# Partial sums of the modulation vectors: an accumulator in SBUF or in a bank of PSUM

## The chip, the cores and the metric

The kernel runs on one core of a Trainium2 chip, as one program in one launch. The metric is the device time of that core in microseconds. A profile is one execution taken by the hardware profiler; its span runs from the first to the last instruction.

## The reference

Two blocks of two layers each work on 256 tokens of width 1024. The second block is conditioned: a vector c of 1024 numbers passes through silu and is multiplied by `ada_w` (1024 x 6144 for each layer), which gives six modulation vectors of 1024 for each layer:

```python
mod = (c_act @ ada_w[l] + ada_b[l]).reshape(B, 6, D)[:, :, None, :]
sh1, sc1, g1, sh2, sc2, g2 = (mod[:, i] for i in range(6))
h = rmsnorm(x, norm_mix[l]) * (1 + sc1) + sh1
...
x = x + g2 * peer(h, peer_w_q[l], peer_sub_keys[l], peer_u[l], peer_v[l])
```

PEER picks 16 of 16384 experts for each of 8 heads of each token, weighs each by a gate, and returns the weighted sum of the experts' rows of `peer_v`. The kernel computes it densely: activations of all experts by `peer_u`, gates that are zero for most, and then the product with all of `peer_v`.

## The kernel before, in words

**Value phase.** Each PEER layer ends with a phase that multiplies the gated activations (128 slots of 128 experts x 256 tokens, in the SBUF tiles slots and slotb) by the 16384 rows of `peer_v`. It has 128 units of 128 experts. Products are made to nearly float32 accuracy from three passes of rounded halves (hi*whi, hi*wlo, lo*whi). In a unit:

- SyncE loads two units' rows at a time, 1 MB, into one of two raw buffers (line 331), when all readers of the buffer's old content are done;
- ScalarE rounds the rows to hi (128 x 1024, line 159), GpSimd subtracts to give one half of lo in two pieces of 256 columns (line 261), VectorE the other half (line 263, 512 columns); hi and lo have two buffers each, so this runs one unit ahead;
- ScalarE rounds the gated activations to whi, VectorE subtracts to give wlo (helper `split`, line 494), also one unit ahead;
- TensorE runs 12 matmuls of 512 columns (line 2093) into four banks of PSUM that are held for the whole phase (tag mm).

Nothing else on TensorE runs in the phase but a few small products.

**Modulation sums.** The generator `ada` (from line 640) computes 512 columns at a time of `c_act @ ada_w`: SyncE loads 256 rows x 512 columns (512 KB, line 654) into one of four buffers, three loads ahead; VectorE multiplies each 128 x 512 half by the entries of c (one scalar per partition) and adds it to an accumulator of 128 x 512. The first of eight such steps is a plain product (line 677), the other seven add (line 679). Then the accumulator is transposed in blocks of 32 (line 687) and reduced (line 688), and at the end of a call four small matmuls and an addition of the bias finish the vectors:

```python
elif first:
    nc.vector.tensor_scalar(out=acc, in0=x, scalar1=s, scalar2=None, op0=ALU.mult)
else:
    nc.vector.scalar_tensor_tensor(out=acc, in0=x, scalar=s, in1=acc, op0=ALU.mult, op1=ALU.add)
```

The generator `ada_slots` makes three such calls, of 2, 6 and 6 column blocks (14 in all: the last two of the first layer's vectors and all of the second layer's), in the first PEER layer's value phase, from unit 21 on. All their buffers lie in the part of the SBUF tile slots whose experts are already consumed. After them it makes the rotary angles.

**Order.** The order of instructions on each engine is written out by the program: after each unit's matmuls the planner (`tick`) grants the generators 1150 ns, and each `yield` of theirs states what the step before it is taken to cost, 660 ns for a sum. So sums are placed in VectorE's order between the subtractions of successive units, and VectorE executes them in that order.

**Banks of PSUM.** Of eight banks four have the tag mm, two aux, two s. `bank(tag)` gives the next buffer of that tag; an instruction that uses it waits until the readers of its old content are done. In the value phase the aux banks serve the small products of `ada`; the s banks were last used by the gates, in the phase before, and are used next by `back` after the phase.

Of the kernel before, what the change touches and what calls it, by code (L numbers as in the profile page):

```python
# [117 lines left out]
class _Kernel:  # L118
# [592 lines left out]
    def ada_slots(self, l):  # L711

        sl = self.slots
        while self.v_done < 21:
            yield 660.0
        for k, p0, n in ((l - 1, 10, 2), (l, 0, 6), (l, 6, 6)):
            yield from self.ada(k, p0, n, [sl[:, 1024 * i:1024 * (i + 1)] for i in range(4)], sl[:, 4096:4608],
                                sl[:, 4608:5120], sl[:, 5120:5248])
        yield from self.angles(sl)

# [1567 lines left out]
```

## Time and profile before

| | us |
|---|---|
| median of 3 runs | 2355.63 |
| lowest, highest | 2337.91, 2359.87 |
| profiled execution | 2348.06 |
| its span | 2346.3 |

Over the span TensorE is busy 2209.1 us, VectorE 1802.1, GpSimd 1744.4 and ScalarE 1295.0. The value phases lie at about 950 to 1340 us (first layer, the one with modulation sums) and 1975 to 2332 us (second layer). In a row of the profile, `L679 DVE SCALAR_TENSOR_TENSOR slots<-slots,cact` is VectorE's instruction of line 679, which writes a tile of the name slots and reads slots and cact. PE is TensorE, PEld its weight loads, DVE VectorE, ACT ScalarE, POOL GpSimd, SPq the queue of SyncE.

### The profile page before, as it was taken

How to read it: one execution, taken by the hardware profiler on the slowest of the kernel's cores; microseconds unless marked ns; L12 is line 12 of the kernel's file. 1: busy time of each engine (PE TensorE's matmuls, PEld its weight loads, DVE VectorE, ACT ScalarE, POOL GpSimd, SP SyncE). 2: the span in 40 equal slices, each digit the busy share in tenths (PEclk: the TensorE clock that was granted, in tenths of full speed). 3: DMA queues.
4: the chain of work that ended last, by engine and by line, in shares of the span. 5: the costliest groups of instructions: out<-in, count | busy, mean ns of one | idle time of the engine just before them, and what ended most of it. 6: DMA issues, size and time to landing. Idle time of an engine off the chain costs nothing. (4 is left out here: it accounts for less than half of the span.)

```text
span 2346.3 us, 42145 instructions
## 1 busy us (share of the span) xinstructions
PE 2209.1 (94%) x14789; PEld 1970.5 (84%) x14789; DVE 1802.1 (77%) x3502; ACT 1295.0 (55%) x2608; POOL 1744.4 (74%) x2070
## 2 busy tenths in 40 slices
PE   8998997899989999999998988998999999999997
PEld 7777887898989999877676777998889999888886
DVE  5818887578787999688989776697868998555555
ACT  2424674554437888544443554554448887555554
POOL 1107878788999888766675686568899888777776
PEclk9989998999999999999999999999999999999999
DMA  5326755477878877577878533587878876555554
GB/s 162 108 73 220 244 177 181 130 196 150 171 151 166 160 158 154 176 251 266 290 262 279 183 117 99 163 180 145 171 154 164 160 154 153 197 194 190 189 192 142
DMA packets 285583, 414.88 MB, mean 177 GB/s; under 512 B 16490, under 2 KB 217387, under 8 KB 285371
## 3 DMA queue, kind: packets, MB, share of 16 engines
q1 hardware_dynamic: 279722, 405.30, 63.6%
q10 hardware_dynamic: 5648, 6.89, 1.1%
q8 instruction: 116, 1.90, 0.4%
q14 instruction: 97, 0.79, 0.1%
HBM read 408.98 MB, written 3.15 MB: 176 GB/s over the span
## 5 line engine op out<-in xcount | busy, mean ns | idle before, releaser
L261 POOL TENSOR_TENSOR lo<-raw,hi 128x256 fp32r<-128x256 f32 x956 | 887.2, 956 | 401.1 <-ACT hi L159 380.4
L261 POOL TENSOR_TENSOR lo<-uT,hi 128x256 fp32r<-128x256 f32 x1022 | 779.0, 799 | 81.7 <-ACT hi L159 81.2
L159 ACT ACTIVATE hi<-raw 128x1024 fp32r<-128x1024 f32 x380 | 401.7, 1059 | 448.5 <-DMA raw<-in_peer_v 212.1
L2042 PE MATMUL mm<-h,hi 128*128 128x256 f32 x4096 | 530.5, 282 | 19.0 <-ACT hi L159 17.7
L2042 PEld LDWEIGHTS mm<-h,hi 128*128 128x128 f32 x4096 | 504.0, 189 | 23.0 <-ACT hi L159 20.5
L263 DVE TENSOR_TENSOR lo<-raw,hi 128x512 fp32r<-128x512 f32 (+1 forms) x290 | 231.2, 798 | 229.2 <-ACT hi L159 227.9
L231 DVE STREAM_TRANSPOSE uT<-raw 128x1024 f32<-128x1024 f32 x256 | 316.8, 1237 | 103.7 <-POOL lo L261 81.0
L159 ACT ACTIVATE hi<-uT 128x1024 fp32r<-128x1024 f32 x256 | 271.5, 1061 | 213.1 <-DVE uT L231 195.2
L2042 PE MATMUL mm<-h,lo 128*128 128x256 f32 x2048 | 313.1, 289 | 14.6 <-POOL lo L261 11.4
L2093 PE MATMUL mm<-hi,wlo 128*128 128x512 f32 x1024 | 278.7, 393 | 15.5 <-DVE wlo L494 15.5
L2042 PEld LDWEIGHTS mm<-h,lo 128*128 128x128 f32 x2048 | 263.5, 189 | 28.7 <-POOL lo L261 28.3
L2093 PE MATMUL mm<-hi,whi 128*128 128x512 f32 x1024 | 277.8, 392 | 5.4 <-ACT hi L159 4.9
L2093 PE MATMUL mm<-lo,whi 128*128 128x512 f32 x1024 | 276.0, 391 | 2.2 <-POOL lo L261 2.1
L2093 PEld LDWEIGHTS mm<-hi,wlo 128*128 128x128 f32 x1024 | 189.3, 188 | 67.0 <-DVE wlo L494 28.8
L2093 PEld LDWEIGHTS mm<-hi,whi 128*128 128x128 f32 x1024 | 190.8, 188 | 49.9 <-ACT hi L159 8.7
L2093 PEld LDWEIGHTS mm<-lo,whi 128*128 128x128 f32 x1024 | 190.3, 188 | 47.5 <-POOL lo L261 6.3
L406 PE MATMUL mm<-h,hi 128*128 128x258 f32 (+2 forms) x1344 | 208.5, 298 | 18.2 <-ACT h L159 8.9
L406 PEld LDWEIGHTS mm<-h,hi 128*128 128x128 f32 x1344 | 183.5, 198 | 23.4 <-ACT h L159 9.9
L1945 DVE TENSOR_TENSOR B<-sin,ij 128x512 f16<-128x512 bf16 x256 | 183.7, 755 | 0.0
L159 ACT ACTIVATE A<-B,cos 128x128 f32<-128x128 f16 x512 | 168.7, 405 | 0.0
L494 DVE TENSOR_TENSOR wlo<-slots,whi 128x256 fp32r<-128x256 f32 x192 | 163.4, 851 | 0.6
L406 PE MATMUL mm<-h,lo 128*128 128x258 f32 (+2 forms) x672 | 110.6, 299 | 3.8 <-POOL lo L261 3.7
(482 smaller groups left out, 2815.2 us busy)
## 6 DMA issues: line engine op xcount, KB each, us to landing
raw<-in_peer_u SPq DMA_DIRECT2D x512, 256.0 KB
raw<-in_peer_v SPq DMA_DIRECT2D x128, 1024.0 KB
slots<-in_ada_w SPq DMA_DIRECT2D x56, 512.0 KB
scratch<-in_ada_w SPq DMA_DIRECT2D x40, 512.0 KB
raw<-in_sb_w_in SPq DMA_DIRECT2D x32, 512.0 KB
raw<-in_peer_w_q SPq DMA_DIRECT2D x32, 512.0 KB
raw<-in_od_w_in SPq DMA_DIRECT2D x24, 512.0 KB
raw<-in_ab_w_in SPq DMA_DIRECT2D x22, 512.0 KB
```

The costliest lines, as they stand in the source:

```text
L159: self.nc.scalar.activation(out=out, in_=in_, func=getattr(ACTF, func), **kw)
L231: self.nc.vector.transpose(ut.rearrange("p b c e -> p c b e"), src)
L261: nc.gpsimd.tensor_sub(lo[:, sl], src[:, sl], hi[:, sl].bitcast(F32))
L263: nc.vector.tensor_sub(lo[:, n:], src[:, n:], hi[:, n:].bitcast(F32))
L406: nc.tensor.matmul(ps[mm][:, :T], w[:, o:o + P], x[:, j * 4 + kk, :T], start=(j == 0 and n_of[mm] == 1), stop=(j == nu - 1 and n_of[mm] == ...
L494: nc.vector.tensor_sub(lo, src, hi.bitcast(F32))
L1945: nc.vector.tensor_tensor(out=B.rearrange("p j n i -> p j (n i)"), in0=iota4, in1=ij[:, g].rearrange("p n i -> p (n i)").unsqueeze(1).to_b ...
L2042: nc.tensor.matmul(ps[:, :T], w[:, c * P:(c + 1) * P], x[:, c, :], start=(pas == 0 and c == 0), stop=(pas == 2 and c == KC - 1))
L2093: nc.tensor.matmul(outs[t][d], w[:, t * P:(t + 1) * P], v[:, 512 * d:512 * d + 512], start=(i == 0 and pas == 0), stop=(i == P - 1 and pas ...
```

## The change

One argument in `ada_slots`: the accumulator given to `ada` is no longer columns 4096 to 4608 of the tile slots in SBUF, but a bank of PSUM with the tag s, taken anew for each of the three calls. The buffer into which the accumulator is transposed stays in SBUF, as do the loaded weights. Everything else, the order included, is the same.

```diff
         for k, p0, n in ((l - 1, 10, 2), (l, 0, 6), (l, 6, 6)):
-            yield from self.ada(k, p0, n, [sl[:, 1024 * i:1024 * (i + 1)] for i in range(4)], sl[:, 4096:4608],
+            yield from self.ada(k, p0, n, [sl[:, 1024 * i:1024 * (i + 1)] for i in range(4)], self.bank("s"),
                                 sl[:, 4608:5120], sl[:, 5120:5248])
```

## Rows read from the trace of the kernel before

**Rows 1.** windows: stretch in us, its length, busy us (instructions) by engine, clock, transfer share, GB/s
```profile
1100.00:1150.00 50.00, 45.21 (x184) 33.02 (x182) 46.53 (x61) 19.86 (x31) 29.68 (x30) 1.00 0.84 288
2040.00:2090.00 50.00, 50.00 (x223) 41.38 (x222) 29.61 (x38) 25.66 (x38) 39.47 (x39) 1.00 0.59 197
```

**Rows 2.** lines: loads of value rows, 1010 to 1306 and 2010 to 2306 us
```profile
L331 SPq DMA_DIRECT2D raw<-in_peer_v x47: 367/368/368, 1013.6 to 1301.7; - x47
L331 SPq DMA_DIRECT2D raw<-in_peer_v x54: 367/368/368, 2010.3 to 2302.4; - x54
```

**Rows 3.** waits, 1010 to 1306 us: total us, times, longest
```profile
PEld mm L2093 <- DVE wlo L494: 27.2, 35, 2.0
PEld mm L2093 <- ACT hi L159: 8.1, 8, 1.9
ACT hi L159 <- DMA raw<-in_peer_v: 99.5, 33, 6.1
```

**Rows 4.** windows: a stretch of sums without a pause
```profile
1135.00:1185.00 50.00, 46.12 (x201) 34.90 (x200) 49.58 (x63) 21.80 (x32) 33.26 (x35) 1.00 0.74 255
```

**Rows 5.** groups, 1010 to 1306 us: busy us, mean ns, idle before, releaser
```profile
L494 DVE TENSOR_TENSOR wlo<-slots,whi 128x256 fp32r<-128x256 f32 x73 | 52.4, 718 | 0.0
L263 DVE TENSOR_TENSOR lo<-raw,hi 128x512 fp32r<-128x512 f32 x95 | 89.3, 940 | 24.8 <-ACT hi L159 24.8
L679 DVE SCALAR_TENSOR_TENSOR slots<-slots,cact 128x512 f32<-128x512 f32 x98 | 98.5, 1006 | 1.5
L261 POOL TENSOR_TENSOR lo<-raw,hi 128x256 fp32r<-128x256 f32 x192 | 190.2, 1015 | 107.5 <-ACT hi L159 101.0 <-PE mm L2093 4.9 <-PE aux L695 0.4
L677 DVE TENSOR_SCALAR slots<-slots,cact 128x512 f32<-128x512 f32 x14 | 10.1, 725 | 0.0
L687 DVE STREAM_TRANSPOSE slots<-slots 128x512 f32<-128x512 f32 x14 | 9.9, 705 | 0.2
```

**Rows 6.** line 679, 1010 to 1306 us: min/median/max ns, starts
```profile
L679 DVE SCALAR_TENSOR_TENSOR slots<-slots,cact x98: 736/1110/1273, 1026.6 to 1300.0; 128x512 f32<-128x512 f32 x98
```

**Rows 7.** loads of modulation weights; transfers, 1010 to 1306 us: packets, MB, share
```profile
L654 SPq DMA_DIRECT2D slots<-in_ada_w x56: 367/462/1622, 1008.8 to 1282.4; - x56
q1 hardware_dynamic: 28249, 79.60, 77.6%
```

**Rows 8.** groups of VectorE with an input from PSUM, whole span
```profile
L1680 DVE SCALAR_TENSOR_TENSOR odo_lo<-aux,gs,odo_hi 128x512 fp32r<-128x512 f32 x4 | 3.0, 748 | 2.2 <-ACT odo_hi L159 2.2
L1670 DVE TENSOR_TENSOR oo<-s,ors 128x512 f32<-128x512 f32 x4 | 2.8, 691 | 0.1
L1441 DVE SCALAR_TENSOR_TENSOR x<-mm,mod,x 128x256 f32<-128x256 f32 x14 | 6.6, 476 | 11.6 <-PE mm L457 11.6
L1809 DVE COPY b<-mm 128x1 f32<-128x1 f32 x32 | 4.6, 145 | 5.2 <-PE mm L406 5.2
```

**Rows 9.** groups of ScalarE: in place in PSUM; SBUF to SBUF
```profile
L159 ACT ACTIVATE mm<-mm 128x256 f32<-128x256 f32 x4 | 1.5, 369 | 4.0 <-PE mm L2042 4.0
L159 ACT ACTIVATE whi<-slots 128x256 fp32r<-128x256 f32 x192 | 77.1, 401 | 0.0
```

**Rows 10.** second layer's U phase: one window; lines 1981 and 1945, 1700 to 1950 us
```profile
1900.00:1950.00 50.00, 50.00 (x475) 49.40 (x474) 49.98 (x90) 41.67 (x119) 44.93 (x60) 1.00 0.81 159
L1981 DVE SCALAR_TENSOR_TENSOR slots<-aux,slots x28: 397/520/546, 1759.5 to 1946.9; 128x384 f32<-128x384 f32 x11, 128x244 f32<-128x244 f32 x1, 128x256 f32<-128x256 f32 x1, 128x268 f32<-128x268 f32 x1
L1945 DVE TENSOR_TENSOR B<-sin,ij x116: 409/838/968, 1751.7 to 1949.4; 128x512 f16<-128x512 bf16 x116
```

**Rows 11.** groups of the second value phase, 2010 to 2306 us
```profile
L494 DVE TENSOR_TENSOR wlo<-slots,whi 128x256 fp32r<-128x256 f32 x83 | 78.5, 946 | 0.6
L263 DVE TENSOR_TENSOR lo<-raw,hi 128x512 fp32r<-128x512 f32 x108 | 75.8, 702 | 125.4 <-ACT hi L159 125.4
```

**Rows 12.** timeline: start us, us, instruction, idle before and releaser
```profile
1110.95 0.37 SPq L331 DMA_DIRECT2D raw<-in_peer_v  x1
...
1118.47 1.06 ACT L159 ACTIVATE hi<-raw 128x1024 fp32r<-128x1024 f32 x1 [5.48 <-DMA raw<-in_peer_v]
```

## The prediction

> **What bounds the kernel now.** I read the busy times by stretch first, to see where TensorE is not busy, then the pace of the loads, then the waits and the groups of instructions inside the stretch that the change touches. The change touches the value phase of the first PEER layer, while the modulation vectors are summed beside it. The second PEER layer has the same value phase without those sums, and so serves as a control: there TensorE is busy 50.00 of 50 us; in the first it is 45.21 of 50 us, with VectorE at 46.53 [rows 1].
>
> One load of value rows feeds two units, so its pace gives the pace of the phase. 47 loads start between 1013.6 and 1301.7 us: 46 steps, 92 units, 288.1 us, 3.131 us per unit. In the control 54 loads take 292.1 us, 106 units, 2.756 us per unit [rows 2]. Beside the sums the phase loses 92 x 0.375 = 34.5 us. That is all that any relief of VectorE can return here.
>
> The waits say who causes it. TensorE's weight loads wait 27.2 us for wlo (the low half of the gates, VectorE, line 494) and 8.1 us for hi (ScalarE) [rows 3]. So most of the 34.5 us is VectorE being late. In a stretch where sums run without a pause VectorE is busy 49.58 of 50 us [rows 4]: there it is the bound.
>
> What VectorE does per unit stands in the groups [rows 5]: wlo at 718 ns, lo at 940, the accumulating sums of line 679 at 1006 (98 of them), and 14 times a first product at 725 and a transpose at 705. The 98 sums are the largest of these in total, 98.5 us. Their spread is the point: 736 ns at the least, 1110 at the median, 1273 at the most [rows 6], for one shape. The same instruction often takes half as long again. Meanwhile GpSimd's subtractions, which read SBUF twice, run at 1015 ns [rows 5].
>
> The stretch is not uniform. Four loads of the modulation weights take nine planner steps (eight sums and one transpose) of 660 ns, and a unit grants 1150 ns: (1150/660) x 4/9 = 0.774 loads per unit. The 56 loads [rows 7] thus fill 72 units; the other 20 are pauses between the three calls. At the control's pace these 20 take 55.1 us, which leaves (288.1 - 55.1)/72 = 3.236 us for an active unit.
>
> **The change part by part.** The accumulator of each of the three calls moves from columns 4096 to 4608 of the SBUF tile to a bank of PSUM with the tag s. No instruction is added or removed: 14 first products write PSUM, 98 sums read and write it, 14 transposes read it. No DMA moves. The modulation loads wait, as now, on the sums that read their slot, so a faster sum can only issue them sooner.
>
> *The bank.* Three banks are taken from the ring of two. Its earlier users, the gates, are read out before the value phase begins, and the next ones are taken after the planner has drained at its end. I cost the wait at nothing. If a bank were still held, the first product would stop VectorE behind one gate read-out, some 0.5 us as line 1981 takes [rows 10], three times, with the next wlo and lo queued behind it and TensorE waiting for those.
>
> *The sums.* No row shows VectorE writing PSUM, so the price is bounded. The nearest row is line 1680, the same operation on 512 elements with a scalar per partition, one input in PSUM, one in SBUF: 748 ns. A plain product on 512 elements with an input from PSUM (line 1670) takes 691 ns, the low end. For the high end, suppose that reading and writing one bank cannot overlap: line 1441 takes 476 ns for 256 elements, line 1680 748 for 512, 272 ns for 256 elements, so 512 elements written apart cost 544 ns more, 1292 ns in all [rows 8]. I take 750, because the first row differs only in where the output lies, and because ScalarE's pass over a PSUM tile in place takes 369 ns for 256 elements, no more than the 401 of its pass from SBUF to SBUF [rows 9].
>
> Is the instruction then also free of the spread? In the second layer's U phase, with GpSimd busy 44.93 of 50 us, line 1981 reads one input from PSUM and one from SBUF. It takes 397 to 546 ns for 244 to 384 elements, and at the 272 ns per 256 elements found above those 140 elements account for 149 ns, the whole difference. Line 1945 in the same stretch, both inputs from SBUF and a single shape, runs from 409 to 968 ns [rows 10]. So the long executions belong to instructions with two SBUF inputs, and the changed sum has only one.
>
> Sum: 98 x (1006 - 750) = 25.1 us less on VectorE, or 98/72 x 0.256 = 0.348 us per active unit, which falls from 3.236 to 2.888 us. That is still above the control's 2.756, so all of it counts, and TensorE takes over only if another 0.13 us per unit goes.
>
> *First products and transposes.* 14 products go from 725 ns (mean, waits included) to about 691 [rows 5, 8], 0.5 us less; if I compare with an undisturbed one instead they may cost up to 3 us more. The transposes keep their 705 ns; an extra of 50 ns would be 0.7 us. I leave both at nothing; nothing covers them in an active unit, so the 3 us go into the range.
>
> *The other users.* wlo and lo on VectorE could become quicker too, as GpSimd is held up less. But their sum is 1.66 us per unit here and 0.946 + 0.702 = 1.65 us in the control, where no sums run at all [rows 5, 11]. I take no gain; the bound is that TensorE's pace is reached, 34.5 us in all.
>
> *A rule that speaks against it.* Line 1680 from PSUM (748 ns) stands against 736 for the quickest all-SBUF sum, and line 1670 (691) against 702 for the control's lo: the rows show 12 ns at most [rows 6, 8, 11]. The Trainium skill, "Perfetto Trace Analysis", section "Optimizing Scalar/DVE Operations", gives VectorE about 60 ns of fixed access time per instruction on SBUF and about 125 on PSUM; an estimate by that page is 65 ns x 126 instructions = 8.2 us of the gain lost, a sum of 17 us.
>
> **The sum.** 25 us off the profiled execution's 2348.06 us gives 2323. That execution lies 7.6 us under the median of the three runs, 2355.63, which themselves span 22 us; against the median the same gain would read 2331.
>
> **The rivals.**
>
> *TensorE's pace is reached.* The relief also shortens wlo, lo and GpSimd's subtractions: 34.5 us, 2314. For it: VectorE would meet GpSimd's subtractions less often. Against: the control's 1.65 us.
>
> *Transfers take over.* The phase moves 79.6 MB at a share of 77.6% [rows 7] over 94.5 units, 0.842 MB per unit; the share at 2.756 us would be 77.6 x 3.131/2.756 = 88%. For an active unit it is worse: 0.524 MB of values and 0.774 x 0.524 of weights, 0.930 MB, at 79.6 MB/(296 us x 0.776) = 347 GB/s needs 2.68 us, 93% of my 2.888. Landings can be slow already: the load issued at 1110.95 was taken up only at 1118.47, 7.5 us later, by a ScalarE that had waited 5.48 us for it [rows 12]. A pair's load starts when the buffer's last reader is done; it is needed two units after that, plus the unit by which ScalarE runs ahead. At 7.5 us per landing it would be late in most pairs. If active units cannot go under 3.1 us, the gain is 72 x 0.136 = 10 us: 2338. Against: most late hi go back to VectorE releasing the buffer late, which the change mends.
>
> *A charge on each access to PSUM.* The three kinds of changed instruction, 126 in all, could pay once more what the shortest instruction with an input from PSUM takes in all, 145 ns [rows 8]: 18.3 us lost of the 25.1, 2341. The pairs of rows above speak against it. The page named there is for a smaller such charge.
>
> *Nothing happens.* If the spread comes from the instruction's place in the order and not from its operands, the sums stay near 1006 ns: 2348. Line 1945 against line 1981 speaks against it.
>
> *Slower.* Reading and writing one bank exclude each other: each sum takes 1292 ns, 98 x 0.286 = 28 us more on the engine that is the bound: 2376. It decides as soon as the mean of line 679 passes 1006 ns. ScalarE's in-place passes are its counter-evidence.
>
> **How the numbers follow.** Chances: VectorE relieved by about 25 us (18 to 31) 0.46, TensorE's pace reached 0.18, transfers take over 0.20, the charge 0.06, nothing 0.06, slower 0.04. About 1% (23.5 us) is what a measurement of this kernel can tell from no change. The forecast's case lies beyond it in somewhat over half of its weight, 0.26; with TensorE's pace that is 0.44, and as the profiled run is under the median, against which the gain reads larger, I say 0.50 for faster. Slower keeps 0.04; the rest, 0.46, is the same. The range runs from 2308 (TensorE's pace and a few us of scatter) to 2344 (transfers take over, and scatter): it leaves out nothing happening, slower, and the edges, under 0.2 together.
>
> **What would show it.** Line 679 near 750 ns with hardly any spread; the pace of the value loads at about 2.9 us per unit; the wait of weight loads for wlo well under 27 us; VectorE no longer at 99% in active stretches. If line 679 stays near 1.0 us, the reading of the spread is wrong. If it falls and the pace does not, and ScalarE's waits for value rows grow past 99.5 us [rows 3], the transfers have taken over. The second value phase should stay at 2.756 us per unit.

## The result and the profile after

The changed kernel takes 2316.72 us (median of 4 runs, 2314.81 to 2320.76) against 2351.02 us (2337.91 to 2359.87, 4 runs) before: a ratio of 0.9876, 95% interval 0.9846 to 0.9907. Timed again beside the last experiment (e8_after_again below) it gave 0.9857, 0.982 to 0.9894. It is 1.2% faster by that ratio; the quotient of the two medians alone would be 0.9854. Its four runs lie within 6 us, those before within 22 (in the later timing 10 and 16).

The profiled execution takes 2316.25 us, 31.8 us less than the one before. Almost all of it comes from one place. The first fence has line 2093 (the matmuls of the value phase, the pass hi*whi) in the changed kernel: least, median and longest ns, then the start of the first and of the last; the first row is the first PEER layer's phase, the second the second layer's. The second fence is the same view of the kernel before.

```profile
L2093 PE MATMUL mm<-hi,whi x512: 387/389/501, 948.2 to 1305.7; 128*128 128x512 f32 x171
...
L2093 PE MATMUL mm<-hi,whi x512: 389/389/793, 1948.1 to 2299.4; 128*128 128x512 f32 x171
```

```profile
L2093 PE MATMUL mm<-hi,whi x512: 387/389/504, 950.3 to 1336.6; 128*128 128x512 f32 x171
...
L2093 PE MATMUL mm<-hi,whi x512: 389/389/793, 1980.0 to 2331.2; 128*128 128x512 f32 x171
```

From first to last start, the first phase took 386.3 us and now takes 357.5; the second took 351.2 and takes 351.3. So 28.8 of the 31.8 us lie in the phase that the change touches, and 6.3 us are left of the 35.1 that it had lost to the second.

By stretch, in the columns of [rows 1]: TensorE is near 50 of 50 us while the sums run, and the transfers' share has gone up to 0.91. VectorE is hardly less busy in the densest stretch, 97% (1090 to 1140 us) where it was 99% [rows 4], because more units now pass in the same time.

```profile
1090.00:1140.00 50.00, 49.55 (x217) 39.88 (x216) 48.47 (x70) 22.86 (x35) 30.72 (x36) 1.00 0.91 331
1100.00:1150.00 50.00, 49.41 (x212) 38.84 (x211) 47.96 (x69) 23.39 (x36) 30.14 (x36) 1.00 0.90 323
1200.00:1250.00 50.00, 50.00 (x222) 41.23 (x220) 45.23 (x69) 24.49 (x36) 33.67 (x37) 1.00 0.91 334
2040.00:2090.00 50.00, 50.00 (x222) 40.67 (x222) 29.25 (x36) 25.68 (x39) 37.97 (x36) 1.00 0.57 198
```

The value loads that answer to [rows 2]: 46 steps, 92 units, (1270.5 - 1011.9)/92 = 2.811 us per unit, where it was 3.131:

```profile
L331 SPq DMA_DIRECT2D raw<-in_peer_v x47: 367/368/368, 1011.9 to 1270.5; - x47
```

The waits in the stretch that answer to [rows 3] (1008 to 1275 us). TensorE's weight loads wait 2.1 us for wlo in place of 27.2. ScalarE's wait for value rows is about what it was:

```profile
ACT hi L159 <- DMA raw<-in_peer_v: 92.5, 38, 4.1
...
PEld mm L2093 <- ACT hi L159: 3.7, 5, 1.1
...
PEld mm L2093 <- POOL lo L261: 2.7, 9, 0.3
PEld mm L2093 <- DVE wlo L494: 2.1, 4, 0.8
```

The groups of the same stretch that answer to [rows 5]:

```profile
L261 POOL TENSOR_TENSOR lo<-raw,hi 128x256 fp32r<-128x256 f32 x192 | 180.2, 963 | 89.3 <-ACT hi L159 81.4 <-PE mm L2093 7.3
...
L263 DVE TENSOR_TENSOR lo<-raw,hi 128x512 fp32r<-128x512 f32 x95 | 84.1, 885 | 32.1 <-ACT hi L159 31.8
L679 DVE SCALAR_TENSOR_TENSOR s<-slots,cact,s 128x512 f32<-128x512 f32 x98 | 73.5, 751 | 1.5
...
L494 DVE TENSOR_TENSOR wlo<-slots,whi 128x256 fp32r<-128x256 f32 x73 | 47.0, 644 | 0.0
...
L677 DVE TENSOR_SCALAR s<-slots,cact 128x512 f32<-128x512 f32 x14 | 10.5, 747 | 0.0
L687 DVE STREAM_TRANSPOSE slots<-s 128x512 f32<-128x512 f32 x14 | 9.9, 710 | 0.2
```

The sums went from 1006 to 751 ns. Their spread, the answer to [rows 6], is gone: 741 to 757.

```profile
L679 DVE SCALAR_TENSOR_TENSOR s<-slots,cact,s x98: 741/750/757, 1025.6 to 1267.7; 128x512 f32<-128x512 f32 x98
```

The transfers, the answer to [rows 7]: the same bytes at a share of 83.1% in place of 77.6%.

```profile
q1 hardware_dynamic: 28266, 79.62, 83.1%
```

### The profile page after: what moved, and what is told of

The parts are those of the page before. It is cut to its first block, busy times and chain, and to the rows that moved or that the text cites. A ratio compares the mean times of both kernels' runs of the same rounds, so it can differ in the third digit from the quotient of the medians.

```text
span 2314.5 us, 42145 instructions
## 1 busy us (share of the span) xinstructions
PE 2194.9 (95%) x14789; PEld 1972.2 (85%) x14789; DVE 1763.1 (76%) x3502; ACT 1292.1 (56%) x2608; POOL 1735.9 (75%) x2070
## 5 line engine op out<-in xcount | busy, mean ns | idle before, releaser
L261 POOL TENSOR_TENSOR lo<-raw,hi 128x256 fp32r<-128x256 f32 x956 | 877.7, 946 | 378.2 <-ACT hi L159 354.7
L263 DVE TENSOR_TENSOR lo<-raw,hi 128x512 fp32r<-128x512 f32 (+1 forms) x290 | 226.0, 780 | 236.5 <-ACT hi L159 235.7
L494 DVE TENSOR_TENSOR wlo<-slots,whi 128x256 fp32r<-128x256 f32 x192 | 158.0, 823 | 0.6
```

The source lines that it names most:

```text
L261: nc.gpsimd.tensor_sub(lo[:, sl], src[:, sl], hi[:, sl].bitcast(F32))
L263: nc.vector.tensor_sub(lo[:, n:], src[:, n:], hi[:, n:].bitcast(F32))
L494: nc.vector.tensor_sub(lo, src, hi.bitcast(F32))
```

## The experiments

The theory: a VectorE instruction with two inputs from SBUF and GpSimd's subtraction, which also reads SBUF twice, hold each other up; one input from PSUM takes the sum out of that. Rivals: the place in the tile slots, the output rather than the inputs, PSUM being quicker for VectorE in itself, and the transfers. In an edit, `nbuf == 4` holds for the three calls of `ada_slots` alone. Every time of a phase below is the distance from the first to the last start of the hi*whi matmuls, as above: 386.3 before, 357.5 after, 351.2 without sums. VectorE's busy time is that between the same two starts.

| kernel | first value phase, us | VectorE busy in it, us | the sums, ns | whole, us |
|---|---|---|---|---|
| before | 386.3 | 326.2 | 1110 median | 2348.06 |
| e0_before_again | 383.7 | 326.3 | 1109 median | 2346.13 |
| e1_own_tile | 382.3 | 325.1 | 1109 median | 2338.34 |
| e5_noloads_sbuf | 377.4 | 324.7 | 1110 median | 2338.74 |
| e7_extra | 364.5 | 307.6 | 748 median | 2329.65 |
| e2_alternate | 364.1 | 304.0 | 742 and 1156 medians | 2321.64 |
| e3_quiet_sbuf | 359.3 | 292.3 | 747 median | 2321.56 (median of 4) |
| after | 357.5 | 290.0 | 750 median | 2316.72 (median of 4) |
| e9_even | 357.0 | 285.1 | 750 median | 2320.57 (median of 4) |
| e4_quiet_psum | 356.4 | 295.4 | 751 median | 2315.00 (median of 4) |
| e8_after_again | 356.3 | 290.7 | 751 median | 2315.80 (median of 4) |
| e6_noloads_psum | 352.1 | 286.2 | 750 median | 2307.77 |

A whole time without a note is one profiled execution. The whole times of single runs differ by more than the phases do (the kernel before alone gave 2338 to 2360 us), so the verdicts rest on the phase and on the instruction.

**e0_before_again**: no edit.

> The kernel before, unchanged, profiled once more, to see how far its own stretch of sums (273.4 us from the first to the last sum, against 242.1 in the changed kernel) varies from run to run. Expected: 265 to 275 us, as the run with the accumulator in another SBUF tile took 267.2; line 679 at about 736/1110/1270 ns.

Phase 383.7 us, 269.4 us from the first to the last sum. So a difference of 3 us between two phases with the accumulator in SBUF says nothing. The two profiles of the changed kernel (after and e8_after_again) differ by 1.2 us.

**e1_own_tile**: SBUF, but not in slots.

```diff
+        own = self.ring.tile([P, 1024], F32, name="own", tag="uT", bufs=2)[:, :512]
...
-            ..., sl[:, 4096:4608],
+            ..., own,
```

> The accumulator stays in SBUF but leaves the tile slots: it lies in a ring buffer (tag uT) that nothing else uses in this phase. Theory (the number of inputs from SBUF decides; two of them make VectorE wait for GpSimd's subtractions): nothing changes, line 679 at about 736/1110/1273 ns, the value loads at 3.13 us per unit, time 2340 to 2360 us. Rival (place: sharing the tile slots with the other work costs the time): line 679 flat near 750 ns, 2.81 us per unit, about 2317 us.

The sums of line 679 (least, median, longest):

```profile
L679 DVE SCALAR_TENSOR_TENSOR own<-slots,cact,own x98: 736/1109/1237, 1024.0 to 1291.2; 128x512 f32<-128x512 f32 x98
```

Nothing changed but 1 to 4 us of the phase, 382.3 for 383.7 and 386.3. Place is out. (Its 2338.34 us is a single run just under what was expected.)

**e2_alternate**: the accumulator goes to and fro between a PSUM bank (index 0) and SBUF (index 1).

```diff
+                elif isinstance(acc, tuple):
+                    i = 2 * k2 + k
+                    if first:
+                        nc.vector.tensor_scalar(out=acc[0], in0=x, ...)
+                    else:
+                        nc.vector.scalar_tensor_tensor(out=acc[i % 2], in0=x, scalar=s, in1=acc[1 - i % 2], ...)
```

> The accumulator alternates: the first product writes PSUM, sums 1, 3, 5, 7 read PSUM and write SBUF (56 in all), sums 2, 4, 6 read SBUF and write PSUM (42). Theory (inputs decide): the 56 run flat near 750 ns although they write SBUF, the 42 spread from 740 to 1270 ns with a mean near 1000 although they write PSUM; the gain is about 56/98 of the whole, 17 us of 29.5 on the stretch, some 2.95 us per unit. Rival (the output decides): the 42 flat, the 56 spread, gain about 42/98. Rival (both must be in PSUM): all 98 spread, no gain.

The two kinds of sums, in turn in VectorE's order. In the second row the weights and the accumulator are both read from the tile slots, which is named once:

```profile
L681 DVE SCALAR_TENSOR_TENSOR slots<-slots,cact,s x56: 732/742/749, 1026.5 to 1276.0; 128x512 f32<-128x512 f32 x56
...
L681 DVE SCALAR_TENSOR_TENSOR s<-slots,cact x42: 746/1156/1241, 1028.7 to 1274.7; 128x512 f32<-128x512 f32 x42
```

The 56 that read PSUM and write SBUF take 732 to 749 ns. The 42 that read SBUF twice and write PSUM take 746 to 1241, with a median of 1156. For the sums, the inputs decide and the output does not matter. The phase is 364.1 us: 22.2 of the 28.8 us, more than the 56/98 that was expected. So the gain is not in proportion to the sums relieved: the last 42 bring 6.6 us. The table says why: VectorE is busy 22.2 us less than before and the phase is 22.2 us shorter, one for one; with the last 42 it is busy 14 us less again, and the phase cannot use more than half of that.

**e3_quiet_sbuf**: the kernel before, with GpSimd out of the first value phase up to its last ten units; VectorE subtracts all of lo.

```diff
-                self.pool_share = 0.5
+                self.pool_share = 0.0 if l == 0 else 0.5
...
+                if l == 0 and i == 118:
+                    self.pool_share = 0.5
```

> Accumulator in SBUF as before, but in the first value phase GpSimd does nothing: VectorE subtracts all 1024 columns of lo. Theory (the spread is the wait for GpSimd): with GpSimd silent line 679 is flat at 736 to 757 ns with both inputs in SBUF, line 494 flat near 415; lo on VectorE costs about 693 + 533 = 1226 ns. VectorE then needs 0.415 + 1.226 + 1.361 x 0.745 + 0.4 = 3.05 us per active unit, less some overlap of neighbours: 2.85 to 3.05 us, a stretch of 260 to 275 us in place of 288, so 2322 to 2337 us although VectorE has taken over all of GpSimd's work. Rival (the spread belongs to the instruction's place or to SBUF itself): sums stay near 1006 ns, VectorE needs 3.6 us per active unit, a stretch of some 310 us, over 2365 us.

```profile
L679 DVE SCALAR_TENSOR_TENSOR slots<-slots,cact x98: 741/747/753, 1032.3 to 1277.6; 128x512 f32<-128x512 f32 x98
```

```profile
L263 DVE TENSOR_TENSOR lo<-raw,hi 128x1024 fp32r<-128x1024 f32 x89 | 108.7, 1221 | 29.3 <-ACT hi L159 28.9
...
L679 DVE SCALAR_TENSOR_TENSOR slots<-slots,cact 128x512 f32<-128x512 f32 x90 | 67.3, 748 | 1.4
...
L494 DVE TENSOR_TENSOR wlo<-slots,whi 128x256 fp32r<-128x256 f32 x75 | 31.3, 418 | 0.0
```

The first fence is line 679 (least, median, longest), the second the groups of VectorE from 1010 to 1260 us (count, busy us, mean ns). With both inputs in SBUF, the sums take 741 to 753 ns once GpSimd is silent, and wlo takes 418 ns where it took 718. So the long executions were waits for GpSimd, and no property of SBUF or of the place.

The start times in the trace of the kernel before say the same of each sum: 58 of the 98 start while a subtraction of GpSimd has more than 0.1 us still to run, and these take 1100 to 1273 ns; the other 40 take 736 to 754. In e2, 36 of the 56 sums that read PSUM start so, and none takes over 749.

One row does not fit the theory as it is worded. The first product of a call's column block has only one such input from SBUF, the weights (c gives one number per partition), and is held up as well. Line 677 before, in e3, and after:

```profile
L677 DVE TENSOR_SCALAR slots<-slots,cact x14: 473/718/1021, 1023.4 to 1285.4; 128x512 f32<-128x512 f32 x14
...
L677 DVE TENSOR_SCALAR slots<-slots,cact x14: 476/479/482, 1028.7 to 1265.0; 128x512 f32<-128x512 f32 x14
...
L677 DVE TENSOR_SCALAR s<-slots,cact x14: 743/747/750, 1022.4 to 1256.2; 128x512 f32<-128x512 f32 x14
```

Before, 6 of the 14 start while a subtraction has more than 0.1 us to run and take 955 to 971 ns; of the others seven take 473 to 480 and one 1021. For this form the output does matter: into PSUM it takes 743 to 750 ns, with GpSimd at work or silent (e4, 745 to 750), which is no wait, but 268 ns more than undisturbed into SBUF. What sets this form apart no run here shows.

The kernel as a whole has a ratio of 0.989 (0.9853 to 0.9927) to the one before: it is faster with GpSimd's help in this phase taken away, for VectorE gets back more in waits than it takes over in work (lo 1221 ns in place of 940).

**e4_quiet_psum**: the same edit on the changed kernel.

> The changed kernel (accumulator in PSUM), and GpSimd does nothing in the first value phase, as in e3_quiet_sbuf. Theory (PSUM helps only by taking the sums out of GpSimd's way): line 679 at 750 ns, the time within 4 us of e3_quiet_sbuf. Rival (PSUM is better for VectorE in itself): some 25 us faster than e3_quiet_sbuf.

```profile
L679 DVE SCALAR_TENSOR_TENSOR s<-slots,cact,s x98: 746/751/758, 1035.8 to 1278.8; 128x512 f32<-128x512 f32 x98
```

751 ns here, 747 in e3: PSUM has no advantage of its own, and costs a sum 4 ns (and a first product the 268 ns above). The phases are 356.4 and 359.3 us, the medians 2315.0 and 2321.6, 6.6 us apart where at most 4 was expected; the ratios, 0.9876 (0.9852 to 0.9899) and 0.989, overlap, so this difference stays open. It is far from 25 us.

**e5_noloads_sbuf** and **e6_noloads_psum**: the kernel before and the changed one, without 44 of the 56 loads of modulation weights.

```diff
-            if n >= 4 * np_:
+            if n >= (nbuf if nbuf == 4 else 4 * np_):
                 return
```

> The kernel before (accumulator in SBUF) with 12 of the 56 loads of modulation weights; the other 44 are left out, and the sums run over what the four buffers hold, so the modulation vectors of these calls are not those of the reference. Same instructions on VectorE. Theory (VectorE with its waits for GpSimd is the bound): the sums keep their spread and the stretch from first to last sum stays at 260 to 273 us. Rival (transfers set the pace): the stretch falls to about 240 us, as far as the changed kernel's.

> The changed kernel with the same 44 loads left out (the modulation vectors of these calls are not those of the reference). Theory (TensorE's pace is nearly reached, transfers have little left to take): the stretch from first to last sum goes from 242.1 to 238 to 242 us. Rival (transfers took over when VectorE was relieved): down by over 5 us, to under 237.

In e5 the sums keep their spread:

```profile
L679 DVE SCALAR_TENSOR_TENSOR slots<-slots,cact x98: 736/1110/1237, 1028.7 to 1292.7; 128x512 f32<-128x512 f32 x98
```

The stretch from first to last sum takes 264.0 us where the kernels with the accumulator in SBUF and all loads had 273.4 (before), 269.4 (e0) and 267.2 (e1): 3 to 9 us from the transfers, not 30. In e6 the stretch falls to 236.2 us. That is under the 237 that I had set as the rival's mark, so by that mark the rival came true: most of the little that the change left (6.3 us of the phase, 5.1 in e8) belongs to the loads of modulation weights. Its first phase, in the view of line 2093 used above:

```profile
L2093 PE MATMUL mm<-hi,whi x512: 387/389/507, 946.0 to 1298.1; 128*128 128x512 f32 x171
```

352.1 us, within 1 us of the phase without sums (one run). TensorE hardly waits any more (1023 to 1259 us):

```profile
ACT hi L159 <- DMA raw<-in_peer_v: 49.6, 26, 3.6
...
PEld mm L2093 <- POOL lo L261: 0.6, 1, 0.6
PEld mm L2093 <- ACT hi L159: 0.2, 1, 0.2
...
PE mm L2093 <- POOL lo L261: 0.2, 1, 0.2
```

**e7_extra**: the changed kernel, with a short copy after every sum.

```diff
                     nc.vector.scalar_tensor_tensor(out=acc, in0=x, ...)
+                if nbuf == 4:
+                    nc.vector.tensor_copy(self.slots[:, 4096:4160], acc[:, :64])
```

> The changed kernel with one more VectorE instruction after each of the 98 sums: a copy of 64 columns of the accumulator from PSUM to a free place in SBUF, about 200 ns each, 20 us in all, which asks nothing of GpSimd. It tells how near VectorE is to being the bound after the change. Theory (VectorE is still just at the edge): most of it shows, the stretch from first to last sum grows from 242.1 by 13 to 20 us, to 255 to 262. Rival (TensorE sets the pace and VectorE has room): it grows by under 6 us.

```profile
L681 DVE COPY slots<-s x112: 223/224/226, 1028.3 to 1281.5; 128x64 f32<-128x64 f32 x112
```

It ran after the first products too, 112 times at 224 ns, which is 25.1 us: just what the 98 sums had gained, 98 x (1006 - 750) ns, given back as plain work. The stretch from first to last sum grew from 242.1 to 250.0 us and the phase from 357.5 to 364.5: 7 to 8 us, between the two expectations. But VectorE's load did not grow by 25.1 us. The groups of this run (1031 to 1281 us):

```profile
L261 POOL TENSOR_TENSOR lo<-raw,hi 128x256 fp32r<-128x256 f32 x176 | 151.3, 884 | 100.9 <-ACT hi L159 100.6
...
L263 DVE TENSOR_TENSOR lo<-raw,hi 128x512 fp32r<-128x512 f32 x87 | 74.6, 858 | 12.1 <-ACT hi L159 11.8
...
L494 DVE TENSOR_TENSOR wlo<-slots,whi 128x256 fp32r<-128x256 f32 x67 | 40.0, 597 | 0.0
```

VectorE does as many microseconds of sums and copies as before the change, but wlo (597 ns) and lo (858) are shorter still than in the changed kernel (644 and 885), and so are GpSimd's subtractions (884 for 963). So VectorE's busy time in the phase grows by 17.6 us only. The phase of the kernel before, of e2, of e7 and of the changed kernel (columns of [rows 1]; the third number after the length is VectorE's):

```profile
950.30:1336.60 386.30, 363.47 (x1558) 282.01 (x1556) 326.18 (x419) 177.10 (x263) 255.47 (x257) 1.00 0.73 250
949.40:1313.50 364.10, 356.20 (x1557) 284.52 (x1556) 303.99 (x419) 176.04 (x263) 252.86 (x256) 1.00 0.73 265
953.90:1318.40 364.50, 356.02 (x1557) 284.85 (x1556) 307.56 (x531) 177.03 (x263) 232.95 (x257) 1.00 0.74 265
948.20:1305.70 357.50, 353.75 (x1557) 285.75 (x1556) 289.98 (x419) 176.44 (x263) 245.58 (x256) 1.00 0.76 270
```

Against the kernel before, VectorE is busy 18.6 us less in e7 and the phase is 21.8 us shorter. In before, e0, e1, e2 and e7 the phase is 57 to 60 us longer than VectorE's busy time, so in these runs, down to some 304 us, a microsecond off VectorE is about a microsecond off the phase. In after, e8 and e9 the difference is 66 to 72 us: there the phase no longer follows VectorE. (These are runs with GpSimd at work and all loads made.)

**e8_after_again** (no edit) and **e9_even**: sums spread over more units.

```diff
-        cost = 1300.0 if pool else 660.0
+        even = nbuf == 4
+        cost = 1300.0 if pool else 740.0 if even else 660.0
...
-            yield 1320.0
-        yield 4.0 * cost
+            yield 800.0 if even else 1320.0
+        yield 800.0 if even else 4.0 * cost
```

> The changed kernel unchanged, timed again beside the one with evened sums. Expected: 2313 to 2321 us; the first value phase at 355 to 358 us from its first to its last hi*whi product (386.3 in the kernel before, 351.2 in the second value phase).

> The changed kernel with the sums spread more evenly: planner cost of a sum 740 in place of 660 ns, the pauses at the start of each call 3 x 800 + 800 in place of 3 x 1320 + 2640 ns, the same units in all. So 0.69 loads of modulation weights per active unit in place of 0.774. Theory (what the change leaves of the loss, some 6 us, is weight transfers that delay the value rows while they bunch): the first value phase shortens by 2 to 4 us against the changed kernel, to 353 to 355 us; too little for the timing to tell. Rival (VectorE's order, not transfers): no change, 357.

The phases are 356.3 and 357.0 us, the medians 2315.80 and 2320.57, the ratios to the kernel before 0.9857 and 0.9882 (0.9843 to 0.9921). Evening the sums does nothing for the phase: the theory's 353 to 355 did not come, the rival's 357 did. The waits in e9 (1005 to 1290 us) have nonetheless lost those for wlo and kept those for lo and hi:

```profile
ACT hi L159 <- DMA raw<-in_peer_v: 107.5, 46, 4.6
...
PEld mm L2094 <- POOL lo L261: 4.3, 11, 0.6
...
PEld mm L2094 <- ACT hi L159: 3.3, 4, 1.7
```

VectorE is busy 285.1 us in this phase, 5 us less than in the changed kernel, and it gained nothing. So VectorE does not look like the bound any more, though the mark set for this run spoke for it. What is left goes with the loads, as e6 shows; spacing them by a tenth did not help, and how they cost it stays open. No version that makes all loads is measurably faster than the changed kernel.

## Why the prediction was right, point by point

**The whole.** 2323 us was forecast, 2316.72 measured, within 2308 to 2344. What came was 31.8 us between the profiles, 28.8 of them in the phase: inside the 18 to 31 of the likeliest case. But it came about in part as the rival "TensorE's pace is reached" had it, with wlo, lo and GpSimd's subtractions shorter too.

**The bound.** Right: the second value phase as a control gave the size of what could be won, and it held. The phase has come to within 6.3 us of it.

**The bank.** Right: the first products, which take the new banks, show no idle time before them (0.0 us in the row of line 677).

**The sums.** Right: 750 ns was taken from line 1680, 751 was measured, and the spread went. That for the sums the number of inputs from SBUF makes it, read from lines 1981 and 1945, is shown by e2 and e3. The conclusion that long executions belong to instructions with two SBUF inputs was too narrow: the first products have one and waited too.

**First products and transposes.** Costed at nothing, and so it was, though not as argued: the products take 747 ns, not 691, which is 14 x 22 ns = 0.3 us more than before. This is luck: into PSUM they cost 268 ns more than undisturbed into SBUF, 3.8 us in all, and the waits for GpSimd that they lost happened to be nearly as long. The transposes take 710 ns for 705.

**The rule that speaks against it.** The Trainium skill ("Perfetto Trace Analysis", "Optimizing Scalar/DVE Operations") gives VectorE about 60 ns of access per instruction on SBUF and about 125 on PSUM, an estimate of 65 ns more. This case's runs show 4 ns, between 747 in e3 and 751 in e4, for a sum of 512 columns that still has one input in SBUF, and 268 ns for the plain product. Neither is near 65. The measurement decides.

**The other users.** This step failed. I took no gain for wlo and lo, since their sum is the same in the control. The stretch's totals say otherwise: lo went from 940 to 885 ns, wlo from 718 to 644. With 95 of each that is 95 x 0.055 + 95 x 0.074 = 12 us more on VectorE, nearly half as much as the sums themselves; over the whole phase VectorE is busy 36.2 us less (290.0 for 326.2). The control was a bad stand-in: there VectorE stands idle until ScalarE is done, starts lo just ahead of GpSimd, and meets GpSimd with wlo:

```profile
2106.91 0.69 DVE L263 TENSOR_TENSOR lo<-raw,hi 128x512 fp32r<-128x512 f32 x1 [1.15 <-ACT hi L159]
2106.96 2.13 POOL L261 TENSOR_TENSOR lo<-raw,hi 128x256 fp32r<-128x256 f32 x2 [0.59 <-ACT hi L159]
2107.52 0.97 DVE L494 TENSOR_TENSOR wlo<-slots,whi 128x256 fp32r<-128x256 f32 x1
```

So it goes throughout the control (2010 to 2306 us): 102 of 108 lo start less than 0.1 us before a subtraction of GpSimd and take 691 to 694 ns, and all 107 wlo start while one has more than 0.1 us to run and take 776 to 968. Beside the sums VectorE runs late and meets GpSimd at other points: before the change 44 of 95 lo start so, with a mean of 1196 ns, and the other 51 have 687; after it 34 do.

**"All of it counts."** Right for the 25.1 us of the forecast: e2 and e7 lie on the line where a microsecond of VectorE is about one of the phase. But VectorE got back 36.2 us, not 25.1, and that is more than the phase could use; it stopped at 28.8, at what the transfers leave of TensorE's pace. So the forecast came this close partly by luck: 11 us of relief were left out, and 7 of the whole were lost at the limit.

**Transfers.** They did not take over (0.20 was given), and ScalarE's wait for value rows stayed at 92.5 us for 99.5. But the rival named the next limit: without most of the weight loads 4 to 6 us more go (e6 against after and e8).

**Nothing, a charge on PSUM, slower.** All three fell with the 751 ns. Reading and writing the same bank in one instruction costs 9 ns at most that show (751 against 742 in e2, which reads PSUM and writes SBUF). Only the 14 first products paid something for PSUM.

## What to carry to other kernels

When one shape of VectorE instruction shows two durations in a trace while GpSimd works, look whether the long ones start while an instruction of GpSimd is running, and count their inputs from SBUF. Here giving one of a sum's two inputs a home in PSUM took the wait away, whichever memory the output went to, and it also shortened the other instructions that share the wait; an accumulator is the natural candidate, if a bank is free. Do not move an output to PSUM for nothing: the plain product lost 268 ns by it. Before handing half a job to GpSimd, price what it costs VectorE in waits: with the sums in SBUF the phase was faster with GpSimd idle, with the sums in PSUM about the same (356.4 us in e4, 357.5 and 356.3 with GpSimd). The kernel has 56 more such sums at 206 to 402 us, in the tile scratch, which still take 733 to 1670 ns after the change; no version here moved those.

## What the runs showed of the hardware

- A `scalar_tensor_tensor` of VectorE over 512 float32 columns takes 732 to 758 ns undisturbed, for each placement run here: both inputs in SBUF (e3, 747), one in PSUM with the output in SBUF (e2, 742), accumulating in place in PSUM (751).
- Beside GpSimd's subtractions of 256 columns, the form with two inputs from SBUF goes up to 1241 or 1273 ns, some 500 more, when it starts while one of them is running (58 of 98 sums before); its output in PSUM doesn't help (e2, 1156 at the median).
- A `tensor_scalar` over 512 float32 columns with one tensor input from SBUF takes 476 to 482 ns into SBUF with GpSimd silent (e3) and up to 1021 beside its subtractions (before); into PSUM it takes 743 to 750 either way (after, e4).
- Those subtractions of GpSimd fell from 1015 to 963 ns with the accumulator in PSUM, and to 884 in e7.
- GpSimd's half of lo was worth less than nothing beside sums with the accumulator in SBUF: without it the kernel ran at 0.989 of its time, wlo at 418 ns in place of 718.
